# A hybrid decoder layer on one core: attention scores by halves of 64 queries, 192 keys in every second block, in a newly searched order

## The chip, the cores and the metric

The kernel runs on one core of a Trainium2 chip. The core has a matrix engine (TensorE, PE in the profile, with its weight loads as PEld), VectorE (DVE), ScalarE (ACT), GpSimd (POOL) and a queue that issues transfers (SyncE, SP). The metric is the device time of one execution in microseconds; the time before is the median of three runs. One more execution was profiled, and all durations below come from it.

## The reference, cut to what matters

One layer, sequence 2048, width 1024, all in float32. Eight query heads of 64 share two key/value heads; a query sees itself and the 127 positions before it; each head has a sink, a learned logit that takes part in the softmax and is then dropped.

```python
z = rms_norm(x, attn_norm_g) @ w_in            # 1024 -> 512 q, 128 k, 128 v, 3 x 512 gates and conv
q, k = rms_norm(q, q_norm_g), rms_norm(k, k_norm_g)
sc = einsum(q, k) * 64 ** -0.5
mask = (delta >= 0) & (delta < 128) & (kpos >= 0)   # delta = query position - key position
p = softmax(concatenate([where(mask, sc, -1e30), sink]))[..., :-1]
y_attn = einsum(p, v)
y_conv = gate_b * short_conv(gate_c * xc, conv_w)   # 3 taps
x = x + concatenate([rms_norm(y_attn), rms_norm(y_conv)]) @ w_out
x = x + square(relu(rms_norm(x) @ w_up)) @ w_down   # 1024 -> 4096 -> 1024
```

## The kernel before

**Numbers.** Every factor of a product is split into a high part in TensorE's reduced fp32 format and a low part that holds the rest. A product takes three matmuls: high by high, high by low, low by high (`mm3`, lines 278 to 280; L1454 and L1571 in the MLP).

**Stages.** First the projections, attention, convolution and output projection (the mixers) in four chunks of 512 positions, each of four blocks of 128. Then the MLP in two halves, up (L1454) and down (L1571), as a seven-product scheme of 2x2 matrices.

**A block of attention** goes through five steps.

- `qk_transpose`: TensorE turns the four pairs of heads (L697, `ptq`) and the keys (L699, `ptk`). ScalarE writes the high parts and VectorE the low parts into `qt` (L702, L703) and `kw` (L704 to L707). The high part of one head and its low part lie in the two halves of the 128 partitions, so that a single matmul adds two of the three terms. `kw` holds two slots of 128 keys: block b writes slot b % 2, and the other slot still has the block before.
- `softmax`: for each pair of heads and each head j two matmuls (r = 0, 1; L724) of 128 queries against both slots, 256 keys (128 in block 0), into one PSUM bank `psc`. Only 128 of the 256 scores of a query are inside the window: the own block's keys up to the query, and the block before's keys after it. So ScalarE copies the own slot to `sc` (L732), and VectorE puts the other slot's scores over it where the key comes later than the query (`later`, a 128x128 pattern; L735, once per head). Then the maximum with the sink, exponentials, sum and division (L737 to L749).
- `probabilities`: TensorE turns `sc` (L760, `ptp`), ScalarE and VectorE write its high and low parts (L766, L767, `pp`), and GpSimd keeps a second copy with only the own block's keys (L773, two selects of 128x512 for each kv head).
- the value products `po` (L812): per kv head two matmuls with the values of the block before (`vz`) and two with the difference of the two blocks' values (`vd`), which need the selects.
- evacuation, squares and the mean (`pa`, L833) for the norm.

PSUM has four banks for these tiles (tag `at`), three for the large products (`mm`) and one more (`tr`).

**What sets the order.** Each engine runs its instructions in a fixed order that is made when the program is built. A generator `besides` yields the large products of the chunk (`pc`, `px`, `pb`, `pout` of the convolution half, next chunk's `pz`) a few matmuls at a time, and the attention code calls `fill(n)` between its steps to take n of them; the counts are in `FILL[chunk]`. Each piece of attention code also has a priority offset in `PRIO[chunk]`, used through `ahead(i)`, by which its instructions move ahead of or behind the rest; `SOON` is such an offset for the convolution norm. In the MLP the order follows a list of its own.

Of the kernel before, what the change touches and what calls it, by code (L numbers as in the profile page):

```python
# [16 lines left out]
P = 128  # L17
# [65 lines left out]
SOON = 330  # L83
# [21 lines left out]
def hymba_layer(  # L105
# [57 lines left out]
    def zrow(name):  # L163
# [13 lines left out]
    later = const.tile([P, P], I32, name="later")  # L177
    nc.gpsimd.memset(later, 1)
# [309 lines left out]
    g_qk = const.tile([P, 2, DH], F32, name="g_qk")  # L488
    sink = const.tile([P, HEADS], F32, name="sink")
# [4 lines left out]
    def load_gains(part):  # L494
        if not part:
            nc.sync.dma_start(g_qk[:, 0, :], q_norm_g[0].partition_broadcast(P))
            nc.sync.dma_start(g_qk[:, 1, :], k_norm_g[0].partition_broadcast(P))
            nc.sync.dma_start(sink, sinks[0].partition_broadcast(P))
            return
# [137 lines left out]
    with tc.tile_pool(name="mix_small", bufs=1) as mix_small, tc.tile_pool(name="mix", bufs=1) as mix:  # L637
# [51 lines left out]
        def qk_transpose(b, zt):  # L689
# [4 lines left out]
            qt = mix.tile([P, HEADS // 2, 2, P], F32R, tag="qt", name=f"qt_{nm}", bufs=1)  # L694
# [5 lines left out]
            p3 = pt.rearrange("p (j q) -> p j q", j=4)  # L700
            for i, (a, o) in enumerate(((lo, hi), (hi, lo))):
                nc.scalar.copy(qt[a, :, i, :], p3[a])  # L702
                nc.vector.tensor_tensor(qt[o, :, i, :], p3[a], qt[a, :, i, :].bitcast(F32), op=ALU.subtract)  # L703
# [8 lines left out]
        def softmax(b, qt):  # L712
# [3 lines left out]
            nk = (2 if b else 1) * P  # L716
            own = b % 2
            sc = mix.tile([P, HEADS, P], F32, tag="sc", name=f"sc_{nm}", bufs=2)
            for pr in range(HEADS // 2):
                kv = pr * 2 // GQ  # L720
                ps = bank("at", f"psc_{nm}_{pr}").rearrange("p (h s k) -> p h s k", h=2, s=2)
                for j in range(2):
                    for r in range(2):
                        nc.tensor.matmul(  # L724
                            ps[:, j].rearrange("p s k -> p (s k)")[:, :nk],
                            qt[:, pr, j, :],
                            kw[:, r, kv, :, :].rearrange("p s k -> p (s k)")[:, :nk],
                            start=r == 0,
                            stop=r == 1,
                        )  # L730
                s2 = sc[:, pr * 2 : pr * 2 + 2, :]
                nc.scalar.copy(s2, ps[:, :, own, :])  # L732
                for j in range(2):
                    other = ps[:, j, 1 - own, :] if b else neg.to_broadcast([P, P])
                    nc.vector.copy_predicated(s2[:, j, :], later, other)  # L735
# [16 lines left out]
        def values(b, zt, v_before, sc, n_fill, fill):  # L752
# [3 lines left out]
            def probabilities(kv):  # L756

                pt = bank("at", f"ptp_{nm}_{kv}")
                for j in range(GQ):
                    nc.tensor.transpose(pt[:, j * P : (j + 1) * P], sc[:, kv * GQ + j, :], ident)  # L760
# [344 lines left out]
        nsink = const.tile([P, HEADS], F32, name="nsink")  # L1105
        with tc.issue_after(rs0_in):
# [504 lines left out]
```

## Time and profile before

| | us |
|---|---|
| median of three runs (1916.32 to 1916.94) | 1916.41 |
| the profiled execution's own time | 1915.76 |
| span of its first to last instruction | 1914.0 |

By stretch of the span, TensorE's busy time is 33.34 us in the first 35 us (the first chunk's query projection), 655.95 us from 35 to 691.5 us (the mixers), 609.30 us from 691.5 to 1300.8 us (up) and 609.32 us in the rest (down). VectorE is busy for 428.95 us and ScalarE for 302.53 us of the 656.5 us of the mixers. The granted clock is 1.00 throughout.

How to read it: a matmul's own duration holds the passage through the array, which overlaps its neighbours; what a matmul costs is the distance from its start to the next one's start. Rows of merged instructions (x16) and the chain of waits give that distance. Idle time of PEld is time in which the weight loads stood still, which the matmul before may still cover.

### The profile page before, as it was taken

What the parts mean: (1) busy time and instruction counts of PE and PEld (TensorE: products, weight loads), DVE (VectorE), ACT (ScalarE), POOL (GpSimd) and SP (SyncE); (2) the same over time, 40 slices, a digit from 0 to 9 for tenths busy, and PEclk for the clock granted to TensorE, in tenths of its full rate; (3) what the DMA queues carried; (4) which work ended last, traced back from release to release, by engine and by line L of the source; (5) the groups of instructions that cost most, each with busy time, mean ns of one, the idle gap of its engine ahead of it and who ended that gap; (6) DMA issues with size and microseconds to landing.
All of it is one profiled execution on the core that took longest, in us unless ns stands there. A gap on an engine that the chain in (4) does not pass through costs nothing.

```text
span 1914.0 us, 24557 instructions
## 1 busy us (share of the span) xinstructions
PE 1907.9 (100%) x8930; PEld 1591.4 (83%) x8930; DVE 1203.1 (63%) x1857; ACT 828.6 (43%) x1557; POOL 274.4 (14%) x477
## 2 busy tenths in 40 slices
PE   9999999999999999999999999999999999999999
PEld 8888888888888888888888888888888888888887
DVE  5895567448467759998788766666534334457541
ACT  6564245335445346544555555453332332232320
POOL 2123212302221112233101111111000000100000
PEclk9999999999999999999999999999999999999999
DMA  8984854564578688777576544448954456766641
GB/s 300 334 322 119 324 197 177 210 230 160 203 263 281 213 293 245 220 220 243 199 233 214 172 148 156 142 148 315 374 193 151 137 171 222 282 228 212 205 137 55
DMA packets 232793, 413.80 MB, mean 216 GB/s; under 512 B 51673, under 2 KB 136417, under 8 KB 219873
## 3 DMA queue, kind: packets, MB, share of 16 engines
q1 hardware_dynamic: 203840, 336.59, 52.0%
q0 software_dynamic: 15424, 51.40, 6.9%
q10 hardware_dynamic: 13408, 24.26, 3.4%
q8 instruction: 70, 1.15, 0.2%
q14 instruction: 51, 0.41, 0.1%
HBM read 286.35 MB, written 125.83 MB: 215 GB/s over the span
## 4 chain that ended last, share of the span: by engine, by line
PE 99%; DVE 0%; POOL 0%; ACT 0%; issue 0%; DVEq 0%; POOLq 0%
PE d L1571 32%; PE u L1454 32%; PE pout L278 3%; PE pout L280 3%; PE pout L279 3%; PE pz L278 2%; PE pz L280 2%; PE pz L279 2%; PE psc_b L724 2%; PE pb_c L280 2%; PE pb_c L279 2%; PE pb_c L278 2%; PE px_c L278 2%; PE px_c L280 2%; PE px_c L279 2%; PE po_b L812 1%
## 5 line engine op out<-in xcount | busy, mean ns | idle before, releaser
L1571 PE MATMUL d<-op_w,op_f 128*128 128x512 f32 x2691 | 609.5, 389 | 0.0
L1454 PE MATMUL u<-op_x,wop 128*128 128x512 f32 x2688 | 609.4, 389 | 0.0
L1571 PEld LDWEIGHTS d<-op_w,op_f 128*128 128x128 f32 x2691 | 504.8, 188 | 104.7
L1454 PEld LDWEIGHTS u<-op_x,wop 128*128 128x128 f32 x2688 | 504.5, 188 | 104.8
L434 DVE TENSOR_TENSOR op_f<-op_f 128x1024 fp32r<-128x1024 f32 x112 | 136.9, 1224 | 235.7 <-ACT op_f L433 235.2
L433 ACT CAST op_f<-op_f 128x1024 fp32r<-128x1024 f32 x112 | 117.6, 1051 | 353.9 <-DMA op_f<-fop 340.6
L452 ACT CAST wop<-wu 128x512 fp32r<-128x512 f32 x156 | 96.1, 619 | 89.3 <-PE u L1454 86.9
L453 DVE TENSOR_TENSOR wop<-wu,wop 128x512 fp32r<-128x512 f32 x156 | 110.5, 710 | 32.0 <-DMA wu<-in_w_up_dram 17.6
L1190 POOL DMA_DIRECT2D fop<-s x96 | 52.1, 542 | 442.5 <-DVE s L1193 438.1
L1196 DVE TENSOR_TENSOR u<-u,u 128x512 f32<-128x512 f32 x128 | 87.9, 686 | 19.6 <-PE u L1454 19.5
L434 DVE TENSOR_TENSOR op_w<-raw,op_w 128x1024 fp32r<-128x1024 f32 x56 | 68.4, 1222 | 25.6 <-ACT op_w L433 25.6
L433 ACT CAST op_w<-raw 128x1024 fp32r<-128x1024 f32 x56 | 58.8, 1051 | 44.5 <-PE d L1571 22.0
L1202 ACT ACTIVATE u<-u 128x512 f32<-128x512 f32 x64 | 40.5, 632 | 58.1 <-DVE u L1196 56.0
L741 ACT ACTIVATE sc_b<-sc_b,ngm_b 128x128 f32<-128x128 f32 x128 | 49.7, 390 | 29.8 <-DVE ngm_b L738 29.8
L773 POOL TENSOR_SCALAR_AFFINE_SELECT pp_b<-pp_b 128x512 fp32r<-128x512 f32 x60 | 41.3, 701 | 134.1 <-ACT pp_b L766 66.2
L1403 POOL DMA_DIRECT2D wds<-raw x16 | 8.5, 533 | 330.9 <-DVE raw L1401 330.9
L453 DVE TENSOR_TENSOR wop<-wu_s,wop 128x512 fp32r<-128x512 f32 x64 | 45.9, 719 | 11.9 <-ACT wop L452 11.8
L452 ACT CAST wop<-wu_s 128x512 fp32r<-128x512 f32 x64 | 39.4, 619 | 30.2 <-PE u L1454 24.4
L278 PE MATMUL pout<-w_wo,yt_c 128*128 128x512 f32 x128 | 51.4, 402 | 0.0
L280 PE MATMUL pout<-w_wo,yt_c 128*128 128x512 f32 x128 | 51.0, 398 | 0.0
L279 PE MATMUL pout<-w_wo,yt_c 128*128 128x512 f32 x128 | 50.2, 392 | 0.0
L735 DVE COPY_PREDICATED sc_b<-later,psc_b 128x128 f32<-128x128 int32 x120 | 29.5, 297 | 32.5 <-ACT sc_b L732 32.1
(265 smaller groups left out, 3120.9 us busy)
## 6 DMA issues: line engine op xcount, KB each, us to landing
op_f<-fop SPq DMA_DIRECT2D x112, 512.0 KB, 4.4
raw<-in_w_down_dram SPq DMA_DIRECT2D x72, 512.0 KB, 4.0
wu<-in_w_up_dram SPq DMA_DIRECT2D x128, 256.0 KB, 4.0
w_wo<-wo SPq DMA_DIRECT2D x24, 1024.0 KB, 6.6
fop<-s POOLq DMA_DIRECT2D x96, 256.0 KB, 2.7
fop<-u ACTq DMA_DIRECT2D x64, 256.0 KB, 2.8
op_x<-xop SPq DMA_DIRECT2D x28, 512.0 KB, 5.9
w_q<-q SPq DMA_DIRECT2D x12, 1024.0 KB, 6.9
```

Of the source, the lines that this page charges most:

```text
L278: nc.tensor.matmul(ps, st(0), mv(0), start=first, stop=False)
L279: nc.tensor.matmul(ps, st(0), mv(1), start=False, stop=False)
L280: last_sum[0] = nc.tensor.matmul(ps, st(1), mv(0), start=False, stop=last).ins
L433: nc.scalar.copy(op[:, 0], raw)
L434: nc.vector.tensor_tensor(op[:, 1], raw, op[:, 0].bitcast(F32), op=ALU.subtract)
L452: splits.append(nc.scalar.copy(hi, blk).ins)
L453: lows.append(nc.vector.tensor_tensor(lo, blk, hi.bitcast(F32), op=ALU.subtract).ins)
L741: nc.scalar.activation(sc[:, hd, :], sc[:, hd, :], AF.Exp, bias=ngm[:, hd : hd + 1], accum_out=den[:, hd : hd + 1])
L1190: eng.dma_start(fop_dram[tb][ORDER_DOWN.index(i)][n // 2][:, n % 2], b)
L1196: return nc.vector.tensor_tensor(dst, ps, b, op=ALU.add).ins
L1454: nc.tensor.matmul(pt, wops[i][:, a, k, :], xops[tb, p][k // 2][:, b, k % 2, :], start=p not in GOES_ON and k + j == 0, stop=k + j == NB + ...
L1571: nc.tensor.matmul(ps[tb][j][:, cs], fs[tb][:, a, k, j * P : (j + 1) * P], w[:, b, k, cs], start=first and p not in GOES_ON and k + n == 0 ...
```

## The change

**Halves instead of heads.** `qt` is laid out by pair, half of 64 queries, head of the pair, query. A score matmul now takes 64 queries of both heads of a pair as its 128 rows. In odd blocks (slot 0 the block before, slot 1 the own) the first half needs keys 0 to 191 of the two slots and the second half 64 to 255, so these matmuls have 192 columns; in even blocks the slots lie the other way round and the 256 columns stay (128 in block 0). The number of matmuls stays.

**Masks by partition.** A row of `sc` is now a query and a head of the pair, and its second index is the pair and the half. `pick` (two patterns of 64 columns) replaces `later`. In each half, 64 of the 128 score columns are the same for every query, and 64 are chosen: ScalarE copies 256 elements per pair as before, VectorE makes one predicated copy of 2x64 columns per pair instead of two of 128. Block 0 starts from a GpSimd fill of `sc` with -1e30. `sink` is laid out by the same rows (two small GpSimd copies from `nsink`, which is loaded in its place). The transposes of `sc` write two runs of 64 columns, which puts the heads back into the old order, so that nothing changes behind them.

**Order.** `PRIO`, `FILL` and `SOON` have other values.

```diff
-SOON = 330
+SOON = 180
 PRIO = (
-    (60, 0, 160, -10, 30, 0, 20, -10, -20, 30, 0, 300, 0, 0),
+    (40, 0, 240, -10, 30, 0, 80, 60, -20, 30, 240, 20, 0, 0),
...
 FILL = (
...
-    ((27, 6), (9, 9, 5, 6, 3), (6, 7, 7, 5, 5), (8, 13, 8, 7, 8), (11, 3, 10, 1, 2)),
+    ((27, 9), (8, 10, 5, 3, 3), (7, 7, 8, 6, 5), (8, 13, 5, 7, 6), (10, 2, 5, 3, 7)),
...
-    later = const.tile([P, P], I32, name="later")
-    nc.gpsimd.memset(later, 1)
-    nc.gpsimd.affine_select(
-        later, later, pattern=[[1, P]], compare_op=ALU.is_gt, fill=0.0, base=0, channel_multiplier=-1
-    )
+    HQ = P // 2
+    pick = const.tile([P, 2, HQ], I32, name="pick")
+    for i in range(2):
+        nc.gpsimd.memset(pick[:, i, :], i)
+        for rows, base in ((P, HQ), (HQ, 0)):
+            nc.gpsimd.affine_select(
+                pick[:rows, i, :],
...
-            qt = mix.tile([P, HEADS // 2, 2, P], F32R, tag="qt", name=f"qt_{nm}", bufs=1)
+            qt = mix.tile([P, HEADS // 2, 2, 2, HQ], F32R, tag="qt", name=f"qt_{nm}", bufs=1)
...
-                nc.scalar.copy(qt[a, :, i, :], p3[a])
-                nc.vector.tensor_tensor(qt[o, :, i, :], p3[a], qt[a, :, i, :].bitcast(F32), op=ALU.subtract)
+                nc.scalar.copy(qt[a, :, :, i, :], p4[a])
+                nc.vector.tensor_tensor(qt[o, :, :, i, :], p4[a], qt[a, :, :, i, :].bitcast(F32), op=ALU.subtract)
...
+            if not b:
+                nc.gpsimd.memset(sc, NEG)
+            width = 3 * HQ if own else 2 * P
+            keys = [slice(i * HQ, i * HQ + width) if own else slice(0, P if not b else 2 * P) for i in range(2)]
...
-                for j in range(2):
+                for i in range(2):
                     for r in range(2):
+                        n = keys[i].stop - keys[i].start
                         nc.tensor.matmul(
-                            ps[:, j].rearrange("p s k -> p (s k)")[:, :nk],
-                            qt[:, pr, j, :],
-                            kw[:, r, kv, :, :].rearrange("p s k -> p (s k)")[:, :nk],
+                            ps[:, i * width : i * width + n],
+                            qt[:, pr, i].rearrange("p j q -> p (j q)"),
+                            kw[:, r, kv, :, :].rearrange("p s k -> p (s k)")[:, keys[i]],
...
-                nc.scalar.copy(s2, ps[:, :, own, :])
-                for j in range(2):
-                    other = ps[:, j, 1 - own, :] if b else neg.to_broadcast([P, P])
-                    nc.vector.copy_predicated(s2[:, j, :], later, other)
...
+                if b:
+                    nc.scalar.copy(s2, (ps if own else ps[:, P:]).rearrange("p (i k) -> p i k", k=2 * P if own else P)[:, :2, :P])
+                    nc.vector.copy_predicated(s4[:, ::3], pick, p8[:, 2:4] if own else p8[:, ::7])
...
-                    nc.tensor.transpose(pt[:, j * P : (j + 1) * P], sc[:, kv * GQ + j, :], ident)
+                    nc.tensor.transpose(p5[:, j // 2, :, j % 2, :], sc[:, kv * GQ + j, :], ident)
```

**TensorE, scores of block 15** (last chunk; `psc_b15_n` is the bank of pair n, `pt_m` the transposes of the MLP's input, `px_c3` and `pb_c3` convolution products). Before:

```order
L279 MATMUL px_c3_1_1_6192<-h1_h3_4592,w_wx13_0_6107 128x512
L724 MATMUL psc_b15_0_6253<-kw_631,qt_b15_6162 128x256
L280 MATMUL px_c3_1_1_6192<-h0_h3_4591,w_wx13_1_6108 128x512
L724 MATMUL psc_b15_0_6253<-kw_631,qt_b15_6162 128x256 x3
L724 MATMUL psc_b15_1_6261<-kw_631,qt_b15_6162 128x256 x2
L278 MATMUL pb_c3_1_0_6239<-h0_h3_4591,w_wb13_0_6235 128x512
L724 MATMUL psc_b15_1_6261<-kw_631,qt_b15_6162 128x256
```

and now:

```order
L289 MATMUL pb_c3_1_0_6194<-h0_h3_4567,w_wb13_1_6191 128x512
L738 MATMUL psc_b15_0_6221<-kw_640,qt_b15_6138 128x192 x4
L738 MATMUL psc_b15_1_6228<-kw_640,qt_b15_6138 128x192 x4
L738 MATMUL psc_b15_2_6235<-kw_640,qt_b15_6138 128x192 x4
L738 MATMUL psc_b15_3_6242<-kw_640,qt_b15_6138 128x192 x4
L287 MATMUL pb_c3_1_0_6194<-h0_h3_4567,w_wb13_0_6190 128x512
```

The sixteen score matmuls had other products between them and now stand in one run, with 192 columns each.

**TensorE, transposes and value products of block 15**, the last block (`ptp_b15_0` and `_1`: its two kv heads; `po_b15_0` the first kv head's values, reading `pp_b15_0_0` and then the selected copy `pp_b15_0_1`). Before:

```order
L760 MATMUL ptp_b15_0_6597<-ident_222,sc_b15_6252 128x128 x4
L760 MATMUL ptp_b15_1_6608<-ident_222,sc_b15_6252 128x128 x4
L278 MATMUL pout3_0_0_0_6647<-w_wo003_0_6505,at_b12_5845 128x512
L279 MATMUL pout3_0_0_0_6647<-w_wo003_1_6506,at_b12_5845 128x512
L280 MATMUL pout3_0_0_0_6647<-w_wo003_0_6505,at_b12_5845 128x512
L812 MATMUL po_b15_0_6651<-pp_b15_0_0_6602,vz_632 128x512
L278 MATMUL pout3_0_0_0_6647<-w_wo003_0_6505,at_b12_5845 128x512
L279 MATMUL pout3_0_0_0_6647<-w_wo003_1_6506,at_b12_5845 128x512
L812 MATMUL po_b15_0_6651<-pp_b15_0_0_6602,vz_632 128x512
L812 MATMUL po_b15_0_6651<-pp_b15_0_1_6603,vd_633 128x512 x2
```

and now, from the last transpose of the first kv head on:

```order
L779 MATMUL ptp_b15_0_6516<-ident_222,sc_b15_6220 128x2x64
L288 MATMUL pout3_1_1_2_6542<-w_wo113_1_6469,yt_c3_0_0_5798 128x512
L289 MATMUL pout3_1_1_2_6542<-w_wo113_0_6468,yt_c3_0_0_5798 128x512
L287 MATMUL pout3_1_1_2_6542<-w_wo113_0_6468,yt_c3_0_1_5872 128x512
L288 MATMUL pout3_1_1_2_6542<-w_wo113_1_6469,yt_c3_0_1_5872 128x512
L779 MATMUL ptp_b15_1_6527<-ident_222,sc_b15_6220 128x2x64
L289 MATMUL pout3_1_1_2_6542<-w_wo113_0_6468,yt_c3_0_1_5872 128x512
L779 MATMUL ptp_b15_1_6527<-ident_222,sc_b15_6220 128x2x64
L831 MATMUL po_b15_0_6549<-pp_b15_0_0_6521,vz_641 128x512
L779 MATMUL ptp_b15_1_6527<-ident_222,sc_b15_6220 128x2x64
L831 MATMUL po_b15_0_6549<-pp_b15_0_0_6521,vz_641 128x512
L852 MATMUL pa_b14_6500<-mean_242,o_b14_6457 128x1
```

after which one more transpose and the two products with `vd_642` follow. The transposes stood in one run and are now taken singly between products. Between the last transpose of the first kv head and that head's fourth value product there are, in both orders, five other 512-column products, four transposes and three value products; the `pa` of block 14 has come in between.

More of the change, by code (lines that the diff above doesn't have):

```diff
@@ L174, in hymba_layer @@
     )
-    later = const.tile([P, P], I32, name="later")
-    nc.gpsimd.memset(later, 1)
-    nc.gpsimd.affine_select(
-        later, later, pattern=[[1, P]], compare_op=ALU.is_gt, fill=0.0, base=0, channel_multiplier=-1
-    )
+    HQ = P // 2
[5 more added lines that the diff above has]
+                pick[:rows, i, :],
+                pick[:rows, i, :],
+                pattern=[[1, HQ]],
+                compare_op=ALU.is_gt,
+                fill=float(1 - i),
+                base=base,
+                channel_multiplier=-1,
+            )
     neg = const.tile([P, 1], F32, name="neg")
@@ L497, in load_gains @@
             nc.sync.dma_start(g_qk[:, 1, :], k_norm_g[0].partition_broadcast(P))
[L498 removed]
+            nc.sync.dma_start(nsink, sinks[0].partition_broadcast(P))
             return
@@ L1104, in hymba_layer @@
             nc.gpsimd.tensor_scalar(g_qk[:, 0, :], g_qk[:, 0, :], DH**-0.5, None, op0=ALU.mult)
-        nsink = const.tile([P, HEADS], F32, name="nsink")
         with tc.issue_after(rs0_in):
+            for j in range(2):
+                r = slice(j * HQ, (j + 1) * HQ)
+                nc.gpsimd.tensor_copy(
+                    sink[r].rearrange("p (r h) -> p r h", h=2),
+                    nsink[r, j::2][:, :, None].to_broadcast([HQ, HEADS // 2, 2]),
+                )
             nc.gpsimd.tensor_scalar(nsink, sink, -1.0, None, op0=ALU.mult)
```

12 lines of the change are left out of this document (9 added, 3 removed), and 14 rows, old and new, of tables (FILL, PRIO).

## The prediction, made before the changed kernel was run

> **What bounds the kernel now.** I read the page first: the share of each engine, and the chain of work that ended last.
>
> ```profile
> span 1914.0 us, 24557 instructions
> PE 1907.9 (100%) x8930; PEld 1591.4 (83%) x8930; DVE 1203.1 (63%) x1857; ACT 828.6 (43%) x1557; POOL 274.4 (14%) x477
> PE 99%; DVE 0%; POOL 0%; ACT 0%; issue 0%; DVEq 0%; POOLq 0%
> ```
>
> TensorE is never out of work, and the chain that sets the end runs through it alone. So only two things count: how far apart its matmuls start, and the moments in which it waits. Everything on DVE, ACT and POOL counts only where it makes TensorE wait. Next the chain in order of time, whose rows of merged matmuls give the distances from start to start (start, duration, what):
>
> ```profile
> 60.47 1.74 PE psc_b L724 x16
> 79.23 1.91 PE psc_b L724 x16
> 110.14 1.91 PE psc_b L724 x16
> 249.49 0.87 PE ptp_b L760 x8
> 691.53 609.28 PE u L1454 x2688
> 1300.81 609.32 PE d L1571 x2691
> ```
>
> From 691.53 us on it is the MLP, 226.7 ns for each matmul of 512 columns (609.28 / 2688) with no gap anywhere; the change touches nothing there, so 1218.6 us stay. What can move lies in the 656 us of the mixers. The first row is block 0, where a score matmul has 128 columns; the next two are blocks with 256. Sixteen of the former take 1.74 us, 108.8 ns each; sixteen of the latter 1.91 us, 119.4 ns each. Half the columns save 10.6 ns of 119.4. A transpose of 128 columns takes 0.87 / 8 = 109 ns, the same again. There is a floor near 109 ns under every matmul that brings its own weights, and 256 columns lie only just above it.
>
> How much of the mixers is waiting? The view of waits, for PE and then for its weight loads (us in total, times, longest):
>
> ```profile
> PE idle L579 <- POOL ident L172: 1.6, 1, 1.6
> PE po_b L812 <- POOL pp_b L773: 0.4, 1, 0.4
> ```
>
> ```profile
> PEld pt_a L306 <- DVE h_h L311: 0.8, 3, 0.4
> PEld po_b L812 <- POOL pp_b L773: 0.8, 1, 0.8
> PEld pt_m L374 <- DVE xt_m L375: 0.7, 2, 0.5
> PEld pa_b L833 <- issue: 0.7, 2, 0.4
> PEld ptq_b L697 <- ACT sc_b L732: 0.6, 2, 0.3
> PEld pout L278 <- DVE x L963: 0.5, 2, 0.3
> PEld pa_b L833 <- ACT yt_c L898: 0.5, 1, 0.5
> PEld po_b L812 <- DVE pp_b L767: 0.2, 1, 0.2
> PEld pt_a L306 <- DVE ms_b L835: 0.2, 1, 0.2
> ```
>
> The 1.6 us are the start. Past it, PE itself stood still for 0.4 us, and the weight loads for 5.0 us in all (the sum of the nine rows), part of which the matmul before still covered. So all waits that any order of the mixers could remove cost between 0.4 and 5.0 us. I take 2.5: at the largest one, shown below, the weight load stood for 0.8 us and TensorE lost 0.53 us, two thirds of it, and shorter stalls are covered further.
>
> **The change part by part.**
>
> **Score matmuls.** 128 of them (8 odd blocks, 16 each) go from 256 to 192 columns; the other 112 of 256 columns and the 16 of block 0 stay. The trace has no 192. If the cost is a straight line between the two measured points, 192 costs 114.1 ns and saves 5.3 ns x 128 = 0.7 us; if 192 is already on the floor, it saves 10.6 x 128 = 1.4 us; it may save nothing, if the 10.6 ns are not a matter of columns but of block 0; nothing in the rows speaks for a loss. I take 1.0 us, between the first two. The columns alone would promise more: at 226.7 / 512 = 0.443 ns each, 64 columns are 28.3 ns, and 128 matmuls 3.6 us; the first row above speaks against it, since there 128 columns fewer saved 10.6 ns and not 56.7.
>
> [...]
>
> **Masks.** VectorE makes 60 predicated copies instead of 120, ScalarE's copies keep their 256 elements:
>
> ```profile
> L735 DVE COPY_PREDICATED sc_b<-later,psc_b 128x128 f32<-128x128 int32 x120 | 29.5, 297 | 32.5 <-ACT sc_b L732 32.1
> L732 ACT COPY sc_b<-psc_b 128x256 f32<-128x256 f32 x64 | 22.6, 373 | 43.7 <-PE psc_b L724 42.7
> ```
>
> A copy of 2x64 has the same 128 elements per row, so I give it the same 297 ns; that is 60 x 0.297 = 17.8 us less of VectorE, and 4 x 0.297 = 1.2 us off the softmax of each block. I cost it at nothing, because nobody waits for the softmax. Its tightest place is block 4:
>
> ```profile
> 242.55 1.22 DVE L749 TENSOR_TENSOR sc_b<-sc_b,den_b 128x1024 f32<-128x1024 f32 x1
> 249.33 1.03 PE L760 MATMUL ptp_b<-ident,sc_b 128*128 128x128 f32 x8
> ```
>
> The division ends at 243.77 us and the transposes that need it start at 249.33, 5.6 us later. By the new order 67 products of 512 columns lie between the last scores of block 4 and its transposes, where there were 64, so the cover stays; were it gone, each 0.1 us of lateness would cost 0.1 us. Were the strided copies dearer, up to twice, 60 x 0.297 us would come back to VectorE, where there were 17.8 us to give: still nothing on the path.
>
> **`qt` by halves.** The first score matmul of a block now needs both pairs of writes to `qt`, not one. These rows price one write each:
>
> ```profile
> L702 ACT CAST qt_b<-ptq_b 64x512 fp32r<-64x512 f32 x32 | 18.6, 580 | 16.5 <-PE ptq_b L697 8.6 <-DVE qt_b L703 6.7 <-PE psc_b L724 0.8
> L703 DVE TENSOR_TENSOR qt_b<-ptq_b,qt_b 64x512 fp32r<-64x512 f32 x32 | 22.0, 688 | 7.3 <-ACT qt_b L702 6.5
> ```
>
> A chain of 0.58 + 2 x 0.69 = 2.0 us becomes at most 2 x (0.58 + 0.69) = 2.5 us plus the key casts between. The new order leaves at least 21 products of 512 columns and 8 transposes in front (block 3: 21 x 0.227 + 8 x 0.109 = 5.6 us; the shortest before was block 14 with 13, 3.0 us). Cost nothing; if segments of 64 made the writes dearer by half, 3.8 us would still fit.
>
> **Transposes.** They write two runs of 64 columns. No row before has such a target; the bound below is zero, above I take a doubling, 128 x 0.109 = 14 us, and go by the equal column count: zero. But more of them now stand singly between products. What that costs (timeline of PE):
>
> ```profile
> 89.18 0.27 PE L760 MATMUL ptp_b<-ident,sc_b 128*128 128x128 f32 x1
> 89.20 0.48 PE L278 MATMUL pc_c<-h_a,w_wc 128*128 128x512 f32 x1
> 89.52 0.27 PE L760 MATMUL ptp_b<-ident,sc_b 128*128 128x128 f32 x1
> ```
>
> A transpose and a product take 0.34 us (89.18 to 89.52) against 0.109 + 0.227 = 0.336: some 8 ns more. In five more blocks than before (1 and 12 to 15), 40 transposes: +0.3 us.
>
> **The order's waits.** The largest one is at the value products of block 15:
>
> ```profile
> 665.97 1.03 PE L760 MATMUL ptp_b<-ident,sc_b 128*128 128x128 f32 x8
> 666.66 0.59 ACT L766 CAST pp_b<-ptp_b 128x512 fp32r<-128x512 f32 x1 [0.56 <-PE ptp_b L760]
> 667.41 0.68 DVE L767 TENSOR_TENSOR pp_b<-ptp_b,pp_b 128x512 fp32r<-128x512 f32 x1
> 668.16 2.31 POOL L773 TENSOR_SCALAR_AFFINE_SELECT pp_b<-pp_b 128x512 fp32r<-128x512 f32 x3 [0.21 <-DVE pp_b L767]
> 668.48 0.40 PE L812 MATMUL po_b<-pp_b,vd 128*128 128x512 f32 x1
> 669.23 0.50 PE L812 MATMUL po_b<-pp_b,vd 128*128 128x512 f32 x1 [0.36 <-POOL pp_b L773]
> 669.57 0.40 PE L280 MATMUL pout<-w_wo,at_b 128*128 128x512 f32 x1
> ```
>
> ACT, DVE and POOL work in a row, and the fourth product starts 0.75 us after the third instead of 0.23: 0.53 us lost, and 0.1 us more behind it (669.23 to 669.57). The rows of the order show the same work between transposes and this product as before, plus one `pa`: this wait stays. The rest of the 2.5 us is spread over waits on norms and transposes, which the new table moves: the `pa` of block 12 gets 13.7 us of work ahead of it where it had 5.7 (some 60 products against 25), while blocks 5, 6 and 12 now have 3.1 to 3.7 us of work (by the same count, at 0.227 us a product) from the last transposes of the first kv head to its fourth value product, near the 2.9 us that block 15 needed. Some go, some come: I take -0.5 us, within -2.5 and +2.5 (four blocks by 0.63).
>
> **The start.** One more fill on POOL stands before the select that TensorE's first matmul waits for:
>
> ```profile
> 0.85 0.20 POOL L171 MEMSET ident<- 128x128 f32 x1
> 0.99 0.20 POOL L178 MEMSET later<- 128x128 int32 x1
> 1.25 0.28 POOL L172 TENSOR_SCALAR_AFFINE_SELECT ident<-ident 128x128 f32<-128x128 f32 x1
> ```
>
> They follow each other by 0.14 us; two half-size ones instead of one cost up to that, 0.1 us; the fill of block 0's `sc` and the copies of `sink` come long before they are needed.
>
> Sum: -1.0 + 0.3 - 0.5 + 0.1 = -1.1 us. The profiled execution took 1915.76 us (span 1914.0), so it becomes 1914.7; the median of the runs lies 0.65 us above it and becomes 1915.3 us. A difference of 0.2%, 3.8 us, is about what a measurement can tell from none, and this is below it.
>
> **The rivals.** *Columns count in full* (-3.6 instead of -1.0: 1912.7 us). For it: the MLP's matmuls cost what their columns say. Against: 128 columns at 108.8 ns. Chance 0.06; with waits removed it passes 0.2%. *The search found nearly all the waits* (-4.0 instead of -0.5, of at most 5.0: 1911.8 us). For it: two of the long waits on `pa` have more cover. Against: PE itself was idle for only 0.4 us, and the largest wait stays. Chance 0.05. *The value products wait on POOL*: the other side. The select chain of 2.9 us (from 666.3, where the fourth of the eight transposes starts, 665.97 + 3 x 0.109, to 669.23) is outrun wherever less work than that stands between the transposes and the fourth value product; each such block costs up to 0.63 us. By the order four blocks are near it, which gives 1.1 - 2.5, that is 1.4 us slower: 1917.8 us, no change still. It makes the kernel slower by over 0.2% only where (3.8 + 1.1) / 0.63 = 8 blocks wait, or these four for 1.2 us each because ACT, DVE or POOL are held up by the casts of `wop` at that time: 1920.5 us or more. Chance 0.13, of which 0.06 past 0.2%. *Strided transposes* cost 38 ns more each and decide from there: 128 x 38 = 4.9 us, 1920.2 us; at a doubling 1929. Chance 0.04. *Nothing at all is saved* (192 columns cost what 256 do, waits only trade places): 1916.5 us, chance 0.12.
>
> **How the numbers follow.** The forecast has the remaining 0.60. Below 1912.6 us (faster by over 0.2%) lie the second rival, 0.05, and a third of the first with a part of the forecast's own low end, 0.03: 0.08. Above 1920.2 lie 0.06 and 0.04: 0.10. The rest, 0.82, is within 0.2%. The range takes in every saving of the scores but the columns in full with all waits gone, and on the upper side the four waiting blocks: 1912.6 to 1918.9 us. The forecast's own range is 1913.3 to 1917.0 us.
>
> **What would show it.** Right: sixteen scores of an odd block in 1.75 to 1.85 us, of an even one still in 1.91; predicated copies 60 times near 300 ns; the eight transposes in a run still 0.87 us; MLP stages 609.3 us each; waits of weight loads past the start again 3 to 6 us in sum, with `po` on POOL among them. Wrong: sixteen scores in 1.4 us; transposes above 130 ns; a wait of TensorE of over a microsecond in the mixers, on `qt`, `sc` or a weight's transfer.

## The result and the profile after

The changed kernel takes 1921.11 us (median of 13 runs, 1919.66 to 1922.59); the kernel before, run beside it, 1916.45 us (13 runs, 1915.69 to 1918.49). The ratio is 1.002 with a 95% interval of 1.0013 to 1.0028: 4.7 us slower, outside the predicted range. The profiled execution of the changed kernel took 1922.06 us, near the top of its runs, and that of the kernel before 1915.76 us, near the bottom of its own; their difference of 6.3 us is thus larger than that of the medians.

The page of the changed kernel, its span, the engines, and the chain that ended last by engine:

```profile
span 1920.3 us, 24508 instructions
PE 1909.1 (99%) x8930; PEld 1588.0 (83%) x8930; DVE 1194.2 (62%) x1797; ACT 831.3 (43%) x1557; POOL 277.1 (14%) x484
PE 93%; DVE 3%; ACT 1%; DMA 1%; POOL 1%; issue 0%; DVEq 0%; SPq 0%; ACTq 0%; POOLq 0%
```

VectorE has 8.9 us less to do (1203.1 before), and yet the chain of waits now runs through it for 3% of the span, where before TensorE alone had 99%. The rows of that chain that the prediction named (start, distance, what):

```profile
78.78 1.76 PE psc_b L738 x16
289.68 0.87 PE ptp_b L779 x8
383.28 1.91 PE psc_b L738 x16
403.49 1.76 PE psc_b L738 x16
697.45 609.70 PE u L1478 x2688
1307.15 609.32 PE d L1595 x2691
```

Sixteen scores of 192 columns take 1.76 us, of 256 still 1.91: 110 against 119.4 ns, so 128 of them save 1.2 us. A transpose with the split target still takes 109 ns, and the two halves of the MLP stay within 0.5 us of 609.3. So nothing that TensorE does became dearer, and it starts its MLP later all the same: 697.45 against 691.53 us. TensorE's busy time in four stretches from 20 to 700 us (length, busy time and count, granted clock), of the kernel before and then of the changed one:

```profile
20.00:183.00 163.00, 163.00 (x876) 1.00 0.76 271
183.00:353.00 170.00, 170.00 (x876) 1.00 0.60 219
353.00:520.00 167.00, 166.99 (x848) 1.00 0.53 199
520.00:700.00 180.00, 179.46 (x912) 1.00 0.73 258
```

```profile
20.00:183.00 163.00, 162.44 (x866) 1.00 0.76 270
183.00:353.00 170.00, 168.74 (x864) 1.00 0.59 215
353.00:520.00 167.00, 165.47 (x845) 1.00 0.51 194
520.00:700.00 180.00, 177.70 (x908) 1.00 0.72 254
```

TensorE stood still for 0.55 us before and 5.65 us now, a little in every chunk. Idle time is less than what is lost: at the longest wait, shown below, 0.86 us against 1.02, since the row of the product before it is 0.39 us long and the next product could start 0.23 us after it.

Summed over all matmuls after 20 us, the distance from start to start exceeds the floor of its kind (110, 119 and 227 ns for 192, 256 and 512 columns, 109 ns for fewer) by 4.7 us before and by 12.7 us now, 8.0 us more; this sum is called the waits below. Eleven places that lose more than 0.2 us each hold 7.4 of the 12.7 us; before there were three, with 1.0 us.

Less the 1.2 us of the scores, and less 0.5 us ahead of 20 us, the 8.0 us make the 6.3 us by which the span grew. The 0.5 us are not the change's: at the very start the matmuls of both kernels stand farther apart than later, though the views give a clock of 1.00 there too (the first ten, `idle`, of 128 columns, take 2.50 us in each, where ten at 0.109 us from start to start take 1.25), and by how much differs from one profiled execution to the next. The first four products of 512 columns took 1.79 us in the kernel before, 1.17 us in the change and 2.00 us in a kernel below that differs from the change only in the columns of its scores; at 0.227 us from start to start they take 1.07.

On whom TensorE waits (us in all, times, longest):

```profile
PE pt_m L383 <- DVE xt_m L384: 1.8, 3, 0.7
PE pa_b L852 <- DVE o_b L847: 1.6, 2, 0.9
PE psc_b L738 <- DVE kw L717: 0.6, 1, 0.6
PE po_b L831 <- POOL pp_b L792: 0.6, 1, 0.6
PE pt_a L315 <- DVE ms_c L1038: 0.4, 1, 0.4
PE pa_b L852 <- DVE xt_m L384: 0.3, 1, 0.3
```

Nearly all are waits on VectorE, an engine that is busy for 62% of the span. How an engine with that much spare time makes TensorE wait is seen at the longest one, the mean of block 7. First GpSimd, then VectorE, then TensorE in the timeline of the changed kernel:

```profile
357.47 1.98 POOL L202 TENSOR_TENSOR rq_b<-ssq_b,mhalf 128x10 f32<-128x10 f32 x1
```

```profile
359.49 0.83 DVE L694 TENSOR_TENSOR z<-z,rq_b 128x640 f32<-128x640 f32 x1 [2.03 <-POOL rq_b L202]
...
365.72 0.89 DVE L694 TENSOR_TENSOR z<-z,rq_b 128x640 f32<-128x640 f32 x1 [2.22 <-POOL rq_b L202]
366.54 0.41 DVE L846 TENSOR_TENSOR o_b<-o_b 128x256 f32<-128x256 f32 x1
366.87 0.68 DVE L696 TENSOR_TENSOR z<-z,g_qk 128x512 f32<-128x512 f32 x1
367.47 0.28 DVE L847 TENSOR_TENSOR o_b<-o_b 128x128 f32<-128x128 f32 x1
```

```profile
366.65 0.39 PE L289 MATMUL pout<-w_wo,at_b 128*128 128x512 f32 x1
367.89 0.35 PE L852 MATMUL pa_b<-mean,o_b 128*128 128x1 f32 x2 [0.86 <-DVE o_b L847]
```

The reciprocal root of a later block's norm takes GpSimd 1.98 us, and VectorE's next instruction, L694, needs it: VectorE does nothing for 2.03 and then 2.22 us. Behind that instruction in the same queue stand the two short sums of `o_b` (0.41 and 0.28 us) that TensorE needs for `pa`. TensorE starts `pa` 1.24 us after its last product instead of 0.23.

The second kind is in block 2, where nothing blocks VectorE. The new order puts other work between its six writes of `qt` and `kw`; the timeline shows the first and the last of them, and then both halves of the scores:

```profile
99.68 0.68 DVE L713 TENSOR_TENSOR qt_b<-ptq_b,qt_b 64x512 fp32r<-64x512 f32 x1
...
107.86 0.29 DVE L717 TENSOR_TENSOR kw<-ptk_b,kw 64x128 fp32r<-64x128 f32 x1
```

```profile
106.09 1.19 PE L738 MATMUL psc_b<-kw,qt_b 128*128 128x256 f32 x8
...
108.30 0.95 PE L738 MATMUL psc_b<-kw,qt_b 128*128 128x256 f32 x6 [0.56 <-DVE kw L717]
```

The first eight scores, of the first kv head, start without a wait: both writes of `qt` are done at 105.94 us. The other eight need the last write of `kw`. In the kernel before the same six writes ran from 103.64 to 106.79 us with one other instruction between them, and the scores had work ahead of them until 109.98 us:

```profile
103.64 0.68 DVE L703 TENSOR_TENSOR qt_b<-ptq_b,qt_b 64x512 fp32r<-64x512 f32 x1 [0.66 <-ACT qt_b L702]
...
106.50 0.29 DVE L707 TENSOR_TENSOR kw<-ptk_b,kw 64x128 fp32r<-64x128 f32 x1
```

```profile
109.98 1.24 PE L724 MATMUL psc_b<-kw,qt_b 128*128 128x256 f32 x9
```

### The profile page after: what moved, and what is told of

The parts are those of the page before. It is cut to its first block, busy times and chain, and to the rows that moved or that the text cites. A ratio compares the mean times of both kernels' runs of the same rounds, so it can differ in the third digit from the quotient of the medians.

```text
span 1920.3 us, 24508 instructions
## 1 busy us (share of the span) xinstructions
PE 1909.1 (99%) x8930; PEld 1588.0 (83%) x8930; DVE 1194.2 (62%) x1797; ACT 831.3 (43%) x1557; POOL 277.1 (14%) x484
## 3 DMA queue, kind: packets, MB, share of 16 engines
q8 instruction: 70, 1.15, 0.2%
## 4 chain that ended last, share of the span: by engine, by line
PE 93%; DVE 3%; ACT 1%; DMA 1%; POOL 1%; issue 0%; DVEq 0%; SPq 0%; ACTq 0%; POOLq 0%
PE u L1478 32%; PE d L1595 32%; PE pout L287 3%; PE pout L289 3%; PE pout L288 2%; PE pz L288 2%; PE pz L287 2%; PE pz L289 2%; PE po_b L831 1%; PE px_c L287 1%; PE px_c L289 1%; PE px_c L288 1%; PE pc_c L287 1%; PE pc_c L289 1%; PE pc_c L288 1%; PE pb_c L289 1%
## 5 line engine op out<-in xcount | busy, mean ns | idle before, releaser
L1478 PEld LDWEIGHTS u<-op_x,wop 128*128 128x128 f32 x2688 | 504.4, 188 | 105.3 <-issue 0.6
L287 PE MATMUL pout<-w_wo,at_b 128*128 128x512 f32 x124 | 48.8, 393 | 0.0
```

What stands on the lines that cost most here:

```text
L287: nc.tensor.matmul(ps, st(0), mv(0), start=first, stop=False)
L1478: nc.tensor.matmul(pt, wops[i][:, a, k, :], xops[tb, p][k // 2][:, b, k % 2, :], start=p not in GOES_ON and k + j == 0, stop=k + j == NB + ...
```

## The experiments

The theory after the result: each wait is an instruction that TensorE needs, standing behind other work in the queue of VectorE (or GpSimd), and the new tables put it there. The rivals: the halves themselves make the waits (all four writes of `qt` are needed, strided layouts), or the masks do. Idle is TensorE's idle time from 20 to 700 us, 0.55 us before and 5.65 us for the change; where there is one run, its time stands without a ratio (the kernel before beside it: 1916.5 us, and 1916.9 us for the old rows of chunk 1). The kernel before itself took between 1915.4 and 1920.6 us beside these runs, so one run alone can't tell 2 us from nothing; there the trace has to.

| kernel | us (runs) | ratio, interval | idle, us |
|---|---|---|---|
| halves, old tables | 1935.5 (4) | 1.0098 [1.0084, 1.0112] | 12.6 |
| heads, new tables | 1927.0 (5) | 1.0052 [1.0039, 1.0065] | 6.6 |
| halves, 256 keys, new tables | 1922.7 (7) | 1.0028 [1.0017, 1.0039] | 4.5 |
| halves, 256 keys, old tables | 1922.7 (1) | | 6.0 |
| halves, old `PRIO` and `SOON`, new `FILL` | 1926.2 (5) | 1.0048 [1.0035, 1.006] | 10.0 |
| change, one priority back | 1921.8 (1) | | 4.8 |
| change, one step later (`REST`) | 1922.2 (1) | | 5.7 |
| change, six numbers | 1923.7 (5) | 1.0036 [1.0022, 1.005] | 5.7 |
| change, chunk 1 with its old rows | 1923.0 (1) | | 5.1 |
| before, one `FILL` + 1 in chunk 0 | 1917.0 (10) | 0.9998 [0.9989, 1.0008] | 1.6 |
| before, one `FILL` + 1 in chunk 2 | 1916.8 (10) | 0.9998 [0.9988, 1.0008] | 1.7 |
| before, heads of a pair in reverse | 1918.3 (11) | 1.001 [1.0001, 1.0019] | 2.0 |
| before, one mask copy for each pair | 1918.9 (11) | 1.001 [1.0001, 1.0018] | 2.1 |

**Code and tables apart.** The change has two parts, the code and the numbers. Each was put with the other's old part; the numbers go back in the changed kernel as below, and forward by the same lines in the kernel before.

```diff
-SOON = 180
+SOON = 330
-    (40, 0, 240, -10, 30, 0, 80, 60, -20, 30, 240, 20, 0, 0),
+    (60, 0, 160, -10, 30, 0, 20, -10, -20, 30, 0, 300, 0, 0),
...
```

> The halves, masks and 192 columns as in the change, with PRIO, FILL and SOON of before. Theory (the new tables put VectorE and GpSimd work that TensorE waits for behind other work, the scores themselves save 1.2 us): no more waits than before, so 1916.4 - 1.2 + 0.1 = about 1915.3 us, span 1912.5 to 1913.5 us; PE waits for pa, pt_m, psc and pt_a under 0.5 us in sum. Rival (the halves themselves make the waits, since a first score product needs all writes of qt, and the copies and masks come at other times): 1919 us or more whatever the tables, with waits of psc on qt or kw. Second rival (both together, the old tables fit the halves as badly): between 1917 and 1919 us.

> The kernel before (256 columns, two predicated copies per pair) with the PRIO, FILL and SOON of the change. Theory (tables): the waits of the changed kernel come here too, about +6 us, so 1921 to 1924 us, with pa behind the norm of q and k on VectorE and pt_m among the waits. Rival (the halves make the waits): 1916 to 1917 us.

Both are slower than both kernels: 19 us for the halves in the old order, 10 us for the heads in the new one. So the theory's 1915.3 us for the first did not come true, and the rival's waits of `psc` on `qt` or `kw` are only 0.3 us of its idle time; the second is 3 us above the range that the theory gave. The waits of TensorE in the heads with the new tables:

```profile
PE po_b L812 <- POOL pp_b L773: 2.1, 3, 1.1
PE pa_b L833 <- DVE o_b L828: 1.6, 2, 0.9
PE pout L278 <- DVE x L963: 1.1, 1, 1.1
PE psc_b L724 <- DVE kw L707: 0.8, 1, 0.8
```

The two waits on `pa` (1.6 us, longest 0.9) and the one on `kw` are those of the changed kernel, in a kernel that has neither halves nor the new masks. They belong to the tables. Four waits recur in this way: the scores of block 2, the value products of block 3, and `pa` of blocks 3 and 7 cost 0.73, 0.72, 0.86 and 1.02 us in the change (3.3 us in all) and 0.92, 0.72, 0.86 and 1.03 us in the heads. A `pt_a` at 474 us costs 0.58 us in the change and 0.35 us in the heads; one at 462 us, 0.40 us in the change, has no counterpart there. The heads lose time of their own besides: 4.0 us from 131 to 138 us, and 1.7 us in the MLP, which the column of idle time doesn't hold. The old tables on the halves have none of the `pa` pair, but others:

```profile
PE pt_a L315 <- DVE h_h L320: 5.4, 5, 2.3
PE pt_m L383 <- DVE xt_m L384: 4.2, 3, 3.4
PE po_b L831 <- POOL pp_b L792: 1.9, 3, 1.1
```

**The columns.** The changed kernel with 256 keys in every block, its masks reading the same scores from their new places.

```diff
-            width = 3 * HQ if own else 2 * P
-            keys = [slice(i * HQ, i * HQ + width) if own else slice(0, P if not b else 2 * P) for i in range(2)]
+            width = 2 * P
+            keys = [slice(0, P if not b else 2 * P) for i in range(2)]
```

> The changed kernel with 256 keys in every block's score products (all keys of both slots, the needed ones picked out of them); masks, rows by halves and tables as changed. It prices the 64 columns: sixteen scores of an odd block 1.91 us instead of 1.76. Theory (weight loads set the floor): 128 x 9.4 ns = 1.2 us slower than the change, 1922.3 us, if the scheduler leaves the rest of the order about as it is. Rival (columns count in full): 3.6 us slower, 1924.7 us.

TensorE's order is that of the change but for a few places, the waits sum to 11.9 us against 12.7, and sixteen scores of block 1 take 1.91 us where they took 1.76: the columns are worth what the rows say, 1.2 us. The medians, 1.6 us apart, agree with that within their error and can't show it by themselves.

**Which table.** The changed kernel with the old `PRIO` and `SOON` and the new `FILL`.

```diff
-SOON = 180
+SOON = 330
...
-    (30, 10, 0, 320, 80, 10, 60, -20, -20, 120, 280, 120, 0, 0),
+    (160, 80, 0, 10, 0, 0, 20, -20, -20, 0, 0, 120, 0, 0),
```

> The changed kernel with PRIO and SOON of before, the new FILL kept. Theory (the priorities decide what stands ahead on VectorE): most of the 6 us go, 1915 to 1917.5 us, and pa waits under 0.5 us. Rival (the fill counts decide, since they set how much TensorE work covers a chain): 1919 to 1922 us.

Neither the theory's time nor the rival's came true. The kernel lies between the new tables and the old ones, and its sum of waits (17.3 us) does too: the old `FILL` and the old `PRIO` each cost the halves several us.

**Repairs at single waits.** In the change, the convolution's work is put back behind the score step of chunk 0 (`PRIO[0][10]` from 240 to 0); in another kernel `REST` goes from 7 to 9, which puts off the mean of a chunk's last block (`pa`) by two steps of the work besides.

```diff
-    (40, 0, 240, -10, 30, 0, 80, 60, -20, 30, 240, 20, 0, 0),
+    (40, 0, 240, -10, 30, 0, 80, 60, -20, 30, 0, 20, 0, 0),
```

```diff
-REST = 7
+REST = 9
```

> The changed kernel with one number of PRIO back (row 0, entry 10, the convolution's evacuation in the first chunk: 240 to 0). VectorE's six writes for block 2's scores then stand in one run, with no convolution work between them. Theory (the waits are VectorE's order): the waits before block 2's scores (some 1.0 us at 105 to 109 us of the span) go, those of the later chunks (pa near 200 and 367 us, pt_m near 564 and 612 us) stay; about 1 us faster than the change. Rival (a first score product waits because it now needs all four writes of qt): at least half of the 1.0 us stays.

> The changed kernel with REST 9 instead of 7: in the last block of a chunk the mean of squares (pa) is issued later. The scheduler moves it behind six more products in the second and third chunk's end and leaves it where it was in the first's. Theory: the wait of 1.0 us on pa near 367 us goes (6 x 0.227 = 1.4 us more cover), that of 0.9 us near 200 us stays; about 1 us faster than the change. Rival (the chain behind pa is as late, so the wait only moves to the evacuation of pout): the same time, with a new wait of about 1 us on pout within 5 us behind pa.

Each removes its wait, and neither shows the microsecond that was expected of it. With the first, the sixteen scores of block 2 run through without one:

```profile
106.47 2.08 PE L738 MATMUL psc_b<-kw,qt_b 128*128 128x256 f32 x16
```

But 0.85 us come up at 131 to 137 us in its place. With the second, the waits on `o_b` fall from two to one, and 0.70 us come up at 373 us, before a product of the output projection, as its rival had it; the spans are 1920.1 and 1920.5 us against 1920.3. Then five old priorities at the places of the longest waits (the one above among them) together with `REST` 9, six numbers in one kernel:

```diff
-REST = 7
+REST = 9
...
-    (200, 0, 120, 20, 10, 0, -60, 40, 320, 30, 60, 160, 0, 0),
+    (200, 0, 120, 240, 10, 0, -60, 40, 320, 30, 60, 160, 0, 0),
```

> The changed kernel with five numbers of its PRIO set back to those of before (row 0 entries 7 and 10, row 1 entry 2, row 2 entry 8, row 3 entry 3) and REST 9. Theory (each long wait is an instruction that TensorE needs and that stands too far behind on VectorE or POOL): the waits at block 2's scores, on pa near 200, 367 and 609 us and on pt_a near 462 and 474 us shrink by some 3 to 4 us in sum: 1917 to 1918.5 us. Rival (the order is one fitted whole, and any mix of tables is worse): 1921 us or more.

No gain: the sum of waits is 14.2 us against 12.7, with a new one of 1.9 us on `pa` at 640 us. Some 1.7 us of it are no waits: from 474.3 to 477.8 us TensorE ran at half its clock (last section). Without them the sum is about that of the change, and the expected 3 to 4 us did not come. And the whole of chunk 1, its row of `PRIO` and its row of `FILL`, as in the kernel before:

```diff
-    (220, -60, 10, -60, 40, 0, -10, 240, 10, 320, 0, 160, 0, 0),
+    (220, -60, -60, -50, 40, 0, 20, 40, -60, 280, 0, 0, 0, 0),
...
-    ((25, 15), (9, 16, 11, 9, 1), (9, 8, 12, 3, 6), (13, 12, 15, 3, 6), (9, 21, 7, 1, 1)),
+    ((25, 15), (9, 16, 11, 8, 1), (9, 8, 13, 3, 2), (13, 12, 15, 6, 5), (9, 14, 11, 5, 3)),
```

> The changed kernel with the second chunk's rows of PRIO and FILL from before. By the chunks' waits in the traces (second chunk: 2.8 us with the new rows, 1.3 us in the halves with all old tables) it becomes 1.5 us faster, 1919.6 us, if a chunk's waits go by its own rows (theory); the same 1921 us or more, if what the first chunk hands over decides (rival).

A miss: `pa` of block 7 loses less (0.32 for 1.02 us), but some 1.2 us come up behind it at 371 us.

**The layout with the old tables.** Halves with 256 keys everywhere and the tables of the kernel before, so that TensorE has the old matmuls in number and size: the edits of the first and the third experiment together.

> Halves, masks by partition and 256 keys everywhere, with PRIO, FILL and SOON of before. Beside the halves with 192 keys and these tables (1935.5 us). If the shorter score products are what upsets the old order: near 1917 us. If the layout and the masks upset it: 1930 us or more. Theory: the second, since the VectorE work that the masks take away is 15 times what the 64 columns take from TensorE.

With 256 keys the loss is 6 us in the one run, not 19; that layout and masks alone bring the whole of it did not come true, nor that they bring nothing. The waits that came:

```profile
PE psc_b L738 <- DVE qt_b L713: 2.4, 1, 2.4
PE po_b L831 <- POOL pp_b L792: 1.9, 3, 1.1
```

The first is block 14. VectorE stood still for 2.77 us before L397, which overwrites `xt_m` and in the trace is let go by the transfer that stores `xt_m`; the writes of `qt` stand behind. With heads, the first product needs the first pair of writes only; in the kernel before it started at 591.76 us, half a microsecond before the last write was done.

**Is any move of the old tables harmful?** One number up by one, in chunk 0 or in chunk 2 of the kernel before.

```diff
-    ((14, 15), (9, 9, 11, 8, 1), (9, 6, 8, 8, 2), (10, 11, 9, 8, 4), (13, 10, 7, 6, 1)),
+    ((14, 15), (9, 9, 11, 8, 1), (9, 6, 9, 8, 2), (10, 11, 9, 8, 4), (13, 10, 7, 6, 1)),
```

> The kernel before with one number of FILL one higher (first chunk, third block, third count: 8 to 9), nothing else. If the few waits of the kernel before are one searched order's luck (theory): new waits of 1 to 6 us in sum in the first two chunks, 1917.5 to 1922.5 us. If small moves are harmless and the halves are at fault (rival): within 1 us of before.

> The kernel before with another number of FILL one higher (third chunk, second block, third count: 11 to 12), nothing else. Theory and rival as for the first: 1917.5 to 1922.5 us with new waits in the third and fourth chunk, or within 1 us of before.

No: both are the same as before within 0.1%. That the old numbers were so closely fitted that any step from them costs microseconds is not so.

**The need of `qt` alone, and the masks.** Two kernels with the old tables, heads and 256 keys. In the first the order of VectorE and ScalarE stays as before, and TensorE's but for one score matmul. In the second, other than its expectation says, the order moved with the masks: some 120 of TensorE's 8930 matmuls stand elsewhere in its trace, the transposes of block 1 at 119 us among them.

```diff
-                for j in range(2):
+                for j in (1, 0):
                     for r in range(2):
```

> The kernel before, with one difference: in each block and pair the score products of the second head come first, so that, as with halves, the first product needs the last write of qt and not the first pair alone. Its work, its layout, its tables and the rows of VectorE and ScalarE stay; on TensorE one score of one block moves. Theory that the need of all four writes is a cause of its own with the old tables: a wait of 0.4 to 0.7 us on qt before the scores of block 14 (in the run with 256 columns and the old tables 2.4 us were lost there; in the kernel before the first product started 0.5 us before the last write was done), small ones elsewhere; 1917 to 1919 us, ratio 1.0003 to 1.0012. Rival that this need costs nothing, as the prediction had it, and the halves lose with the old tables by what else they change in the queues: no wait on qt at block 14, ratio within 0.0003 of 1.

The wait came where it was expected, and is small. VectorE ends the last write of `qt` of block 14 at 593.89 us, and the first score waits for it:

```profile
593.20 0.69 DVE L703 TENSOR_TENSOR qt_b<-ptq_b,qt_b 64x512 fp32r<-64x512 f32 x1
```

```profile
594.04 0.36 PE L724 MATMUL psc_b<-kw,qt_b 128*128 128x256 f32 x1 [0.25 <-DVE qt_b L703]
```

It costs 0.41 us from start to start. The rest of the 1.2 us is not the edit by this profile: the largest loss, 1.46 us before `ptq` of block 1, stands behind ScalarE's casts of `w_wb`, which began at 61.44 us here and at 59.91 us in the kernel before, on the arrival of weights. The kernels with one `FILL` number changed and the one with the masks have the same order up to there and lose 0.90, 0.27 and 0.60 us at this place, the kernel before none in its profile: this wait too differs from execution to execution.

```diff
-                for j in range(2):
-                    other = ps[:, j, 1 - own, :] if b else neg.to_broadcast([P, P])
-                    nc.vector.copy_predicated(s2[:, j, :], later, other)
+                if b:
+                    nc.vector.copy_predicated(s2, later2, ps[:, :, 1 - own, :])
...
```

> The kernel before with the masks alone changed: one predicated copy of 2 x 128 per pair of heads in place of two of 128 (56 copies fewer, block 0 keeps its eight); scores by heads, 256 keys and the old tables stay, and TensorE's instructions stand in the same order. Each copy should take about 0.43 us (256 elements at a bit over 1 ns and some 0.16 us), so VectorE has 56 x 0.17 = 9 us less to do. Theory that VectorE's order, not its amount, makes TensorE wait: time stays or gets worse by waits at other places, 1916 to 1922 us, ratio 0.9998 to 1.003, and the sum of TensorE's waits does not fall below that of the kernel before. Rival that less VectorE work makes waits fewer: 0.5 to 1.5 us faster.

The page and the group of its copies:

```profile
PE 1908.9 (100%) x8930; PEld 1591.0 (83%) x8930; DVE 1198.2 (63%) x1797; ACT 828.8 (43%) x1557; POOL 278.4 (15%) x479
L735 DVE COPY_PREDICATED sc_b<-later,psc_b 128x256 f32<-128x256 int32 x60 | 24.9, 442 | 34.4 <-ACT sc_b L733 34.0
```

VectorE has 4.9 us less to do than in the kernel before (I had expected 9; a copy takes 442 ns, near the 0.43 us of the estimate, which goes with the rows of VectorE shown above: 0.28, 0.41 and 0.68 us for 128, 256 and 512 elements, that is 1.04 ns for an element and 0.15 us besides), and nothing was gained: 0.1% slower, idle 2.1 us against 0.55. Since the order moved too, this is the price of the masks with what the scheduler made of them, not of the masks alone. Its largest wait is again block 14's `qt`, but that one can't be laid to the masks, as the next place shows.

**A wait that differs from execution to execution.** The kernel with one number of `FILL` changed in chunk 2 has the same instructions in the same order as the kernel before in chunk 3, where block 14 is. Its VectorE and TensorE there:

```profile
590.02 0.69 DVE L388 TENSOR_TENSOR xt_m<-xt_m,xt_m 128x512 f32<-128x512 f32 x1 [2.20 <-DMA xop<-xt_m]
```

```profile
594.18 0.50 PE L724 MATMUL psc_b<-kw,qt_b 128*128 128x256 f32 x2 [0.77 <-DVE qt_b L703]
```

The same instruction waited 0.53 us in the kernel before, 1.51 us with one mask copy for each pair, and 2.77 us in the halves with 256 keys. By these four waits, 0.53 to 2.77 us, the store lets go of `xt_m` earlier or later by some 2 us, and VectorE's queue hands that on: 1.35 us lost on block 14's scores here, in a kernel whose median is no slower. So waits on `qt` at block 14, and part of those on `pt_m` from 560 to 612 us in the change (0.87, 0.57 and 0.82 us in its profile; 1.15, 0.53 and none with 256 keys), are not fixed by the order alone, while the four that recur in the heads, and the `pt_a` at 462 us, came back there with the same length (0.74, 0.72, 0.87, 1.02 and 0.40 us).

## Why the prediction was wrong

*The scores*: right; 1.2 us saved for 1.0, inside the bounds of 0.7 to 1.4. 192 columns take 110 ns, close to the 108.8 and 109 ns of 128 and below the 114.1 of the straight line, and 256 columns cost 9.4 ns more. That the weight loads set this floor, as the third experiment's theory has it, is inferred from the trace and was not tried by itself: in the change the loads of sixteen such scores follow each other without a pause (1.98 us from 78.39 us on), while in the up half of the MLP, at 227 ns a product, they stand still for 39 ns per load (105.3 us over 2688).

*The masks*: right in the price of one copy (298 ns) and in effect, no wait of TensorE on `sc`. The 17.8 us of VectorE work to be saved were too many: it was 8.9 us, since copies in a row overlap (three of them fill 0.69 us in the trace, not 0.9). *The transposes*: 109 ns, right; the rival that made them dearer falls. *The MLP and the start*: right (TensorE's first wait is 1.6 us as before).

*`qt` by halves costs nothing*: nearly right in the changed kernel, but by a wrong argument. The step compared the products in front of the scores with a chain of writes of 2.5 us and the key casts. In block 2, with 31 products in front in both kernels, the first and the last of the writes began 8.2 us apart (99.68 and 107.86), since the tables put other VectorE work between them. The wait was on `kw`, 0.6 us idle, and the heads have it too with these tables (0.8 us); `qt` was in time. With the old tables the need of the last write of `qt` costs 0.4 us at block 14 by itself.

*The order's waits, -0.5 us within 2.5 either way*: this is the step that failed. It measured +8.0 us between the two profiles; from the medians about +5.9 us (4.7 slower and 1.2 saved). The profiles overstate it, since that of the kernel before is of one of its best executions, without waits that its near copies show. Two things in it were wrong. The range was taken from what could be gained: the waits that the trace of before still had, and four blocks at the value products. What a new order can lose is not bounded by those; the kernel before had hardly any waits left, so nearly every new one was a loss. And the step read only TensorE's rows, by how much work stands ahead of an instruction there. The lost time came through the rows of VectorE: `o_b` behind a norm that waits for GpSimd, `kw` behind the convolution, `xt_m` behind the softmax. That 3.3 us of it come with the tables alone is shown by the heads with the new tables; which part of the rest comes with the tables, with the halves or with the single execution is not shown.

*The rival on the slower side* had the sign and, by luck, the size (1920.5 us or more), but the wrong place: the value products cost 0.72 us in block 3 and 0.34 in block 15, not 0.6 in eight blocks. The test it came with, a wait of over a microsecond on `qt`, `sc` or a weight, would have missed the cause: the longest idle time is 0.9 us, on `pa`, and the loss is the sum of a dozen.

*Open*: whether some table gives the halves as few waits as the heads have in theirs, which would be worth some 1.2 us below the kernel before; none that was tried comes near. Why 192 keys lose 13 us more than 256 in the old order was not settled: the profile shows other waits, behind an order that moved, and the clock below. The two sums of waits are 24.5 and 12.2 us; some 5 us of the difference are the half clock, an estimate from the distances between the matmuls in it, less their floors and the idle time.

## What to carry to other kernels

Where one engine is nearly always busy and the order is fixed, look for a change's price in the queues of the engines that feed it: for each instruction that the busy engine needs, ask what stands ahead of it there and whether that waits for a third engine or a transfer (here the two sums of `o_b`, 0.41 and 0.28 us, stood behind a wait of 2.22 us for GpSimd, and TensorE lost 1.02 us). The waits left in a trace bound what a new order can gain, and say nothing of what it can lose. A table of order is fitted to one code; when code and table change together, run each with the other's old half before crediting either.

## What was not expected of the hardware

In two of the kernels TensorE ran at half its clock for some microseconds, by the granted clock of their views (0.50 in the first). The longest time was in the halves with the old tables, after a cluster of waits (stretch, busy time and count, granted clock):

```profile
478.00:479.20 1.20, 0.14 (x2) 1.00 0.00 0
479.20:481.20 2.00, 1.13 (x10) 1.00 0.19 57
481.20:482.20 1.00, 1.00 (x5) 0.52 0.83 324
485.00:487.80 2.80, 2.80 (x7) 0.50 0.62 199
```

Products of 512 columns then start 0.43 us apart instead of 0.227 and the clock is back at 488.1 us: some 7 us at half speed, whose cost comes on top of the waits. The same kernel has it from 146.7 to 150.2 us, after a wait of 2.3 us (0.96, 0.50 and 0.98 in the 3 us from 144, 147 and 150 us on), and the change with six numbers back from 474.3 to 477.8 us, after a wait of 0.50 us alone (0.72 and 0.71 in the 3 us from 473 and 476 us on, with TensorE busy for 2.50 of the first 3). The length of a wait alone does not decide it: TensorE was busy for 0.14 and 1.13 us in the 3.2 us ahead of the first, while one lone wait of 3.4 us in the same kernel, the longest on `pt_m` above, left the clock at 1.00. What decides between them was not tried.
